# Splitting the last tile of the last product of a two-layer decoder step into two halves of the tokens

## The chip, the cores and the metric

One core of one Trainium2 chip. The metric is the device time of one execution of the program in microseconds; of several runs the median is given.

## The reference

One inference step of two decoder layers, for a prompt of 256 tokens and 8 single-token samples that share all weights: 264 tokens of 1,024 features. Each layer has a normed input projection, a mixer (attention beside a gating or pooling part), an output projection, and then a convolutional feed-forward with 2,816 inner features. A final norm follows. What matters here is the end of it:

```python
def rmsnorm(x, g):
    xf = x.astype(jnp.float32)
    y = xf * lax.rsqrt(jnp.mean(xf * xf, axis=-1, keepdims=True) + EPS)
    return (y * g).astype(x.dtype)

def conv_ffn(x, prev, norm_g, w_gate, w_up, conv_w, conv_b, w_down):
    ...
    a = jax.nn.gelu(gc) * (h @ w_up)
    return x + a @ w_down, g_all[:, -(CONV_W - 1):]
...
    y_prompt = rmsnorm(xp, final_norm)
    y_sample = rmsnorm(xs, final_norm)
```

The norm is over a token's 1,024 features, so no token needs another one's sum.

## The kernel before, in words

Features lie on the 128 partitions and tokens along the free axis. `X` holds the residual stream as 8 tiles (`KD`) of 128 features by 264 tokens (`T`). Every weight product runs through `run` (L310): the weights are 128x128 blocks, in the order of use that `_phases` writes down, and `run` walks this order. A block is loaded as part of a chunk of 16 (`raw`, L275, three chunks in the air on SP's queue), and 8 blocks at a time are split by `split` (L290) into a high and a low part of type fp32r: ScalarE copies `wh` (L306), VectorE subtracts to get `wl` (L307), three groups of 8 ahead of their use. Activations are split the same way. Each pair of output tile `m` and inner block `k` costs three matmuls of 264 columns, high by high, high by low and low by high (L329 to L331), which add up in one PSUM tile; when a tile's last block is done, `evac` is called.

The last product is `dn1`, the feed-forward's second product of layer 1: 8 output tiles of 128 features, each with 22 inner blocks (`NF`), one tile after the other. Its right-hand side is `act`, which is complete when `dn1` starts. Its `evac` is the one of `residual(..., operand=False)` (L566): VectorE adds the tile to `X` (L572), ScalarE squares it (`sq`, L386), GpSimd adds the squares up in `acc_fin` (L398), and ScalarE multiplies the tile by the final gain (L577). The last tile's square isn't added to `acc_fin`; `Norm.finish` hands both to `rstd_of` (L403), where two matmuls with a matrix of ones sum over the partitions (L406, in plain fp32, which the trace shows as two passes each) and ScalarE takes Ln and Exp (L408, L409) to get `R`, the reciprocal root for each token. Then five multiplications by `R` on VectorE (L1022), of 1, 2, 2, 2 and 1 tiles (`YD`), each with a store of its tiles behind it (L1023), in turn from SP's and ScalarE's queue.

Tiles come from pools that turn over (`sm`, `up`, and `psm` with four PSUM tiles for products). A scheduler orders each engine's instructions by its own estimate of times; so an engine's order isn't simply that of the text, but within an engine the queue is then fixed.

Of the kernel before, what the change touches and what calls it, by code (L numbers as in the profile page):

```python
# [9 lines left out]
F32 = mybir.dt.float32  # L10
# [3 lines left out]
AF = mybir.ActivationFunctionType  # L14
ALU = mybir.AluOpType
# [3 lines left out]
P = 128  # L19
D = 1024  # L20
KD = D // P
SEQ = 256
NS = 8
T = SEQ + NS
HD = 64
NH = 8
PAST = 256
# [4 lines left out]
NF = DFF // P  # L32
# [7 lines left out]
SQL = 2  # L40
XD = (1, 2, 4, 8)
WARM = 8
YD = ((0, 1), (1, 3), (3, 5), (5, 7), (7, 8))

SC0 = 9
SGL = 6
# [30 lines left out]
NEG = -1e30  # L77
SCALE = HD ** -0.5
POOLW = (2, 4, 8, 16)
# [91 lines left out]
def _consts():  # L171
# [13 lines left out]
    c, s = np.cos(ang.astype(np.float64)).astype(f), np.sin(ang.astype(np.float64)).astype(f)  # L185
    C, S = np.ones((P, T), f), np.zeros((P, T), f)
    for b in (0, 64):
# [20 lines left out]
_INS = [  # L208
    ("w", (_NB * P * P,)), ("x", (P, KD + KD * T)), ("vec", (P, _NVEC)), ("cst", _CST_ARR.shape), ("rope", (P, 2 * T)),
    ("kt0", (NPHYS, P, 512)), ("vp0", (NPHYS, P, 512)), ("kt1", (NPHYS, P, 512)), ("vp1", (NPHYS, P, 512)),  # L210
# [1 line left out]
    ("sguw", (P, 512)), ("sgub", (P, 512)), ("poolw", (P, 512)),  # L212
]
_OUTS = [
    ("y", (KD, P, T)), ("k0", (P, 4, T)), ("v0", (P, 4, T)), ("bvn", (P, 4, NS)),
    ("k1", (P, 4, T)), ("v1", (P, 4, T)), ("poolp", (P, 4, NST)), ("pools", (P, 4, NS, NST)),
    ("cv0", (P, NF, 10)), ("cv1", (P, NF, 10)), ("cs0", (P, NF, NS)), ("cs1", (P, NF, NS)),
]
# [3 lines left out]
def tile_decoder_step(ctx: ExitStack, tc: tile.TileContext, a):  # L222
    nc = tc.nc
    v, s, g, pe = nc.vector, nc.scalar, nc.gpsimd, nc.tensor
# [6 lines left out]
    sm = ctx.enter_context(tc.tile_pool(name="sm", bufs=3))  # L231
    psm = ctx.enter_context(tc.tile_pool(name="psm", bufs=MMB, space=PSUM))
    psa = ctx.enter_context(tc.tile_pool(name="psa", bufs=8 - MMB, space=PSUM))

    def f4(name, shape=(P, 4, T), dt=F32):
        return up.tile(list(shape), dt, tag="u", name=name)
# [4 lines left out]
    def hl(tiles, k):  # L241
        return tiles[k // 4][0][:, k % 4, :], tiles[k // 4][1][:, k % 4, :]

    def at(name):
        return psa.tile([P, 512], F32, tag="at", name=name)

    XG = con.tile([P, KD + KD * T], F32, name="XG")
    GAIN = XG[:, :KD]
    X = XG[:, KD:].rearrange("p (m t) -> p m t", t=T)
# [7 lines left out]
    def vec(n):  # L257
        o, w = _VEC[n]
        return VEC[:, o:o + w]
# [28 lines left out]
    pos = [0]  # L288

    def split(t):  # L290
        for tt in range(len(splits), min(t + (LOOK if pos[0] else 0), NT - 1) + 1):
            ci = chunk_of[tt]
            for c in range(ci, min(ci + 3, len(_CHUNKS))):
                raw(c)
            o = (tt * 8 - coff[ci]) * P
            src = raws[ci][:, o:o + 8 * P]
            h = wsp.tile([P, 8 * P], F32R, tag="wh", name=f"wh{tt}")
            l = wsp.tile([P, 8 * P], F32R, tag="wl", name=f"wl{tt}")
            splits[tt] = (h, l)
            if tt == 0:  # L300
                def piece(c, e, h=h, l=l, src=src):
                    c, e = c * P, e * P
                    tc.keep_in_program_order(v.tensor_copy(h[:, c:e], src[:, c:e]))
                    tc.keep_in_program_order(v.tensor_tensor(l[:, c:e], src[:, c:e], h[:, c:e].bitcast(F32), ALU.subtract))
                return piece
            s.activation(h, src, AF.Copy)  # L306
            v.tensor_tensor(l, src, h.bitcast(F32), ALU.subtract)  # L307
        return splits[t]

    def run(order, rhs, evac, hooks=None):  # L310
        hooks = sorted((hooks or {}).items())
        n = 0
        seen, left, ps = {}, {}, {}
        for m, k in order:
            left[m] = left.get(m, 0) + 1
        for m, k in order:
            i = pos[0]
            pos[0] += 1
            h, l = split(i // 8)
            c = (i % 8) * P  # L320
            if m not in ps:
                ps[m] = psm.tile([P, 512], F32, tag="mm", name=f"mm{i}")
                first = True
            else:
                first = False
            left[m] -= 1
            o = ps[m][:, :T]
            xh, xl = rhs(m, k)
            pe.matmul(o, h[:, c:c + P], xh, start=first, stop=False)  # L329
            pe.matmul(o, h[:, c:c + P], xl, start=False, stop=False)  # L330
            pe.matmul(o, l[:, c:c + P], xh, start=False, stop=left[m] == 0)  # L331
            if left[m] == 0:
                evac(m, o)
            n += 1
            while hooks and n >= 8 * (hooks[0][0] + 1):
                for f in hooks.pop(0)[1]:
                    f()

    orders = dict(_PHASES)


# [21 lines left out]
    ones = con.tile([P, P], F32, name="ones")  # L363
# [3 lines left out]
    epst = con.tile([P, 1], F32, name="epst")  # L367
# [32 lines left out]
        def finish(self):  # L400
            return rstd_of([self.acc] + self.last, 1.0 / D, self.name)

    def rstd_of(parts, scale, name):  # L403
        p = at(f"ns_{name}")
        for i, x in enumerate(parts):
            pe.matmul(p[:, :T], ones, x, start=i == 0, stop=i == len(parts) - 1)  # L406
        R = sm.tile([P, T], F32, tag="R", name=f"R_{name}", bufs=2)
        s.activation(R, p[:, :T], AF.Ln, bias=epst, scale=scale)  # L408
        s.activation(R, R, AF.Exp, scale=-0.5)  # L409
        return R  # L410

# [102 lines left out]
        g.tensor_tensor(C0[:, l], C0[:, l], t, ALU.add)  # L514
        nc.sync.dma_start(a[f"cs{l}"], CSTATE[:, l, :, 1, :])

    def ffn(l, xg, R, down_evac, hooks=None):
        cw, cb = vec("cw"), vec("cb")
        wc = lambda i, j: cw[:, (l * 3 + i) * NF + j:(l * 3 + i) * NF + j + 1]
        cvo = sm.tile([P, NF, 10], F32, tag="cvo", name=f"cvo{l}", bufs=1)  # L520
        act = [mv(f"a{l}_{i}") for i in range((NF + 3) // 4)]
        xn = [mv(f"xn{l}{i}") for i in range(2)]
        gain = vec(f"f{l}")
        half = {}

        def normalise(m):
            z = sm.tile([P, T], F32, tag="rz", name=f"xr{l}{m}", bufs=2)
            g.tensor_tensor(z, X[:, m, :], R, ALU.mult)
            operand_tile(xn[m // 4], m, z, gain[:, m:m + 1])

        def evac(m, o):
            n, j = m
            if n == "g":
                wk = f4(f"wk{l}_{j}", (P, 2, T))
                C = wk[:, 0, :]
                if j < JN:
                    G = wk[:, 1, :]
                    v.tensor_tensor(G, o, R, ALU.mult)
                else:
                    G = o  # L540
                s.activation(C, G, AF.Identity, scale=wc(2, j), bias=cb[:, l * NF + j:l * NF + j + 1])
                v.scalar_tensor_tensor(C[:, 1:SEQ], G[:, 0:SEQ - 1], wc(1, j), C[:, 1:SEQ], ALU.mult, ALU.add)  # L542
                v.scalar_tensor_tensor(C[:, 2:SEQ], G[:, 0:SEQ - 2], wc(0, j), C[:, 2:SEQ], ALU.mult, ALU.add)
                v.tensor_tensor(C[:, SEQ:T], C[:, SEQ:T], C0[:, l, j, :], ALU.add)
                s.activation(cvo[:, j, :], G[:, SEQ - 2:T], AF.Copy)
                s.activation(C, C, AF.Gelu_apprx_tanh)
                half[j] = wk
            else:
                wk = half.pop(j)
                C, A = wk[:, 0, :], wk[:, 1, :]  # L550
                if j < JN:
                    v.tensor_tensor(A, o, R, ALU.mult)
                    g.tensor_tensor(A, A, C, ALU.mult)  # L553
                else:
                    v.tensor_tensor(A, o, C, ALU.mult)
                halves(*hl(act, j), A)

        hk = Hooks()
        for m in range(KD):
            hk.at(NA + NB_ * m, normalise, m)  # L560
        run(orders[f"ff{l}"], lambda m, k: hl(xg if m[1] < JN else xn, k), evac, hk)
        nc.sync.dma_start(a[f"cv{l}"], cvo)
        lnexp()
        run(orders[f"dn{l}"], lambda m, k: hl(act, k), down_evac, hooks)

    def residual(gain, name, operand=True):  # L566
        xg = [mv(f"xg_{name}{i}") for i in range(2)] if operand else None
# [19 lines left out]
    xg = [mv(f"xg_0{i}") for i in range(2)]  # L587
    nrm = Norm("n0", True)
# [17 lines left out]
    R = nrm.finish()  # L606
# [236 lines left out]
    xg, nrm, evac = residual(vec("f0"), "f0")  # L843
    run(orders["out0"], pick([catA, catB]), evac, hk)
    R = nrm.finish()
    gelu_set()
    xg1, nrm1, evac = residual(vec("n1"), "n1")
# [9 lines left out]
    xg, R = xg1, nrm1.finish()  # L857
# [155 lines left out]
    xg, nrm, evac = residual(vec("f1"), "f1")  # L1013
    run(orders["out1"], pick([catA, catB]), evac, hk)
    R = nrm.finish()
    gelu_set()
    _, nrm, evac = residual(vec("fin"), "fin", operand=False)
    ffn(1, xg, R, evac)
    R = nrm.finish()
    for i, (m, e) in enumerate(YD):  # L1020
        x = X[:, m:e, :]
        v.tensor_tensor(x, x, R.unsqueeze(1).to_broadcast([P, e - m, T]), ALU.mult)  # L1022
        (s if i % 2 else nc.sync).dma_start(a["y"][m:e].rearrange("m p t -> p m t"), x)  # L1023


def _lay(inp):
# [62 lines left out]
```

## Time and profile before

| | |
|---|---|
| three runs | 617.85, 618.89, 619.99 us |
| median | 618.89 us |
| profiled execution | 618.47 us |
| its span, from first to last instruction | 616.4 us |
| granted TensorE clock, mean of the span | 0.996 |
| moved by DMA in the span | 121.40 MB |

The profile is of one execution. A page gives the busy time of each engine (PE is TensorE's matmuls, PEld its weight loads, DVE VectorE, ACT ScalarE, POOL GpSimd, SPq and ACTq the queues of SP and ScalarE), the chain of work that ended last, followed back from the last instruction, and the costliest groups of instructions. Other views list instructions in order of time, group them by line and shape, or give each engine's busy time in a stretch. A matmul's duration in the profile includes the way through the array; matmuls overlap, so the pace is read from start to start.

### The profile page before, as it was taken

To read this page: it belongs to the slowest core of one execution; us is meant where nothing else is said; L and a number is where in the kernel's file an instruction comes from. 1 tells how busy PE (TensorE), PEld (TensorE's weight loads), DVE (VectorE), ACT (ScalarE), POOL (GpSimd) and SP (SyncE) were. 2 spreads that over 40 slices of the span, in tenths; PEclk is the share of its full clock that TensorE was granted. 3 is DMA by queue.
4 is the path that set the end of the run, shared out by engine and by line. 5 is a ranking of instruction groups with operands and counts; after the bars stand their busy time and mean duration, and the time that the engine had idled before them with its cause. 6 is when DMAs were issued, how large, how long until landed. Compare 5 with 4: busy or idle time off the path is not lost.

```text
span 616.4 us, 12351 instructions
## 1 busy us (share of the span) xinstructions
PE 599.4 (97%) x4924; PEld 575.3 (93%) x4924; DVE 413.1 (67%) x704; ACT 350.4 (57%) x621; POOL 84.9 (14%) x111
## 2 busy tenths in 40 slices
PE   7899999999999999999999999999999999999994
PEld 5788987999999999999999997899999999999994
DVE  6986663969976676655555686396996766764441
ACT  5459763767756555644442757376765555554441
POOL 3330132324200000001110000042420000001020
PEclk9999999999999999999999999999999999999998
DMA  7995873543655445695477559944364555554502
GB/s 259 325 403 220 328 258 54 206 153 133 216 184 205 158 184 205 228 392 200 155 229 262 219 184 141 134 175 172 136 215 170 200 182 167 199 189 166 200 1 70
DMA packets 41354, 121.40 MB, mean 197 GB/s; under 512 B 17490, under 2 KB 19410, under 8 KB 29906
## 3 DMA queue, kind: packets, MB, share of 16 engines
q1 hardware_dynamic: 40178, 119.00, 59.3%
q10 hardware_dynamic: 1120, 1.63, 0.9%
q8 instruction: 38, 0.62, 0.4%
q14 instruction: 18, 0.15, 0.1%
HBM read 116.67 MB, written 3.94 MB: 196 GB/s over the span
## 4 chain that ended last, share of the span: by engine, by line
PE 84%; DVE 7%; issue 3%; DMA 2%; ACT 2%; POOL 1%; SPq 0%; DVEq 0%; ACTq 0%
PE mm L330 26%; PE mm L329 25%; PE mm L331 25%; DMA raw<-in_w 2%; DVE wl L307 2%; DVE xn_l L374 1%; PE pv_l L465 1%; PE sc L451 1%; PE pav L494 1%; PE Z L900 1%; DVE wk L542 1%; ACT wh L306 1%; PE Z L884 1%; POOL wk L553 0%; PE pt L684 0%
## 5 line engine op out<-in xcount | busy, mean ns | idle before, releaser
L307 DVE TENSOR_TENSOR wl<-raw,wh 128x1024 fp32r<-128x1024 f32 x183 | 229.4, 1255 | 129.1 <-ACT wh L306 129.0
L306 ACT ACTIVATE wh<-raw 128x1024 fp32r<-128x1024 f32 x183 | 193.7, 1059 | 182.5 <-PE mm L330 169.3
L330 PE MATMUL mm<-xn_l,wh 128*128 128x264 f32 x544 | 154.7, 284 | 1.7 <-DVE xn_l L374 1.5
L329 PE MATMUL mm<-xn_h,wh 128*128 128x264 f32 x544 | 153.8, 283 | 0.0
L331 PE MATMUL mm<-xn_h,wl 128*128 128x264 f32 x544 | 153.4, 283 | 0.0
L330 PEld LDWEIGHTS mm<-xn_l,wh 128*128 128x128 f32 x544 | 102.3, 188 | 2.5 <-DVE xn_l L374 2.5
L329 PEld LDWEIGHTS mm<-xn_h,wh 128*128 128x128 f32 x544 | 102.1, 188 | 0.0
L331 PEld LDWEIGHTS mm<-xn_h,wl 128*128 128x128 f32 x544 | 102.1, 188 | 0.0
L330 PE MATMUL mm<-a_l,wh 128*128 128x264 f32 x352 | 99.8, 284 | 0.0
L329 PE MATMUL mm<-a_h,wh 128*128 128x264 f32 x352 | 99.5, 284 | 0.0
L331 PE MATMUL mm<-a_h,wl 128*128 128x264 f32 x352 | 99.4, 283 | 0.0
L331 PEld LDWEIGHTS mm<-a_h,wl 128*128 128x128 f32 x352 | 66.2, 188 | 0.0
L330 PEld LDWEIGHTS mm<-a_l,wh 128*128 128x128 f32 x352 | 66.2, 188 | 0.0
L329 PEld LDWEIGHTS mm<-a_h,wh 128*128 128x128 f32 x352 | 66.0, 188 | 0.0
L329 PE MATMUL mm<-xg_h,wh 128*128 128x264 f32 x160 | 46.6, 298 | 3.6 <-DVE q L637 1.6
L330 PE MATMUL mm<-xg_l,wh 128*128 128x264 f32 x160 | 46.1, 293 | 0.0
L331 PE MATMUL mm<-xg_h,wl 128*128 128x264 f32 x160 | 44.7, 291 | 1.3 <-DVE wl L307 1.3
L329 PE MATMUL mm<-xg_f_h,wh 128*128 128x264 f32 x160 | 45.8, 286 | 0.0
L330 PE MATMUL mm<-xg_f_l,wh 128*128 128x264 f32 x160 | 45.4, 284 | 0.0
L331 PE MATMUL mm<-xg_f_h,wl 128*128 128x264 f32 x160 | 45.3, 283 | 0.0
L329 PE MATMUL mm<-xg_n_h,wh 128*128 128x264 f32 x128 | 37.4, 292 | 0.0
L331 PE MATMUL mm<-xg_n_h,wl 128*128 128x264 f32 x128 | 36.8, 288 | 0.0
(266 smaller groups left out, 1074.5 us busy)
## 6 DMA issues: line engine op xcount, KB each, us to landing
raw<-in_w SPq DMA_DIRECT2D x89, 1024.0 KB, 4.8
K<-in_kt SPq DMA_DIRECT2D x32, 256.0 KB, 6.0
V<-in_vp SPq DMA_DIRECT2D x32, 256.0 KB, 5.6
raw<-in_w SPq DMA_DIRECT2D x5, 512.0 KB, 5.3
CST<-in_cst SPq DMA_DIRECT2D x1, 548.0 KB, 5.5
XG<-in_x ACTq DMA_DIRECT2D x1, 528.0 KB, 7.8
out_k<-k SPq DMA_DIRECT2D x1, 528.0 KB, 9.4
out_v<-v SPq DMA_DIRECT2D x1, 528.0 KB, 3.0
```

Of the source, the lines that this page charges most:

```text
L306: s.activation(h, src, AF.Copy)
L307: v.tensor_tensor(l, src, h.bitcast(F32), ALU.subtract)
L329: pe.matmul(o, h[:, c:c + P], xh, start=first, stop=False)
L330: pe.matmul(o, h[:, c:c + P], xl, start=False, stop=False)
L331: pe.matmul(o, l[:, c:c + P], xh, start=False, stop=left[m] == 0)
L374: j = v.scalar_tensor_tensor(l, src, gain, h.bitcast(F32), ALU.mult, ALU.subtract)
L451: pe.matmul(ps[32 * t:32 * t + 32, :PAST].rearrange("p (g k) -> p g k", g=NPG), qz[:, t, sq, :], kt[sq][:, :, t * P:(t + 1) * P], start=sq ...
L465: pe.matmul(pv[32 * j:32 * j + 32, :], pz[:, pg, sq, :], vtiles[sq][:, pg, :], start=pg == 0, stop=pg == NPG - 1)
L494: pe.matmul(o, vt[:, 0, h * HD:(h + 1) * HD], w[:, :SEQ], start=True, stop=False)
L542: v.scalar_tensor_tensor(C[:, 1:SEQ], G[:, 0:SEQ - 1], wc(1, j), C[:, 1:SEQ], ALU.mult, ALU.add)
L884: tc.keep_in_program_order(pe.matmul(ps[:, 0:SEQ], kh[:, 0:P], qh[:, 0:SEQ], start=False, stop=False, skip_group_check=True))
L900: pe.matmul(ps[:, 0:384], negU, x, start=False, stop=False, skip_group_check=True)
```

## The change

The last tile of `dn1` (its 22 blocks) leaves `run` and goes through a new function, twice: once for tokens 0 to 131 and once for tokens 132 to 263 (`HT` = 132). Each half has a PSUM tile of its own, its own add, square and gain, its own sum over partitions and `R`, and its own four multiplications and stores. In the first half the square and `acc` are added on VectorE before one sum; in the second the sum takes both, as before. The multiplications write to a new tile `Y` instead of in place, two feature tiles of 132 tokens at a time (264 elements for a partition), and the output `y` is laid out so that a store's piece for one partition, two tiles by 132 tokens, is contiguous.

```diff
+HT = T // 2
-YD = ((0, 1), (1, 3), (3, 5), (5, 7), (7, 8))
+YD = ((0, 2), (2, 4), (4, 6), (6, 8))
-    ("y", (KD, P, T)), ("k0", (P, 4, T)), ("v0", (P, 4, T)), ("bvn", (P, 4, NS)),
+    ("y", (2, P, KD, HT)), ("k0", (P, 4, T)), ("v0", (P, 4, T)), ("bvn", (P, 4, NS)),
+    def run_last(order, rhs, evac):
+        base = pos[0]
+        pos[0] += len(order)
+        for hf in range(2):
+            a_, b_ = hf * HT, (hf + 1) * HT
+            ps = psm.tile([P, 512], F32, tag="mm", name=f"last{hf}")
+            o = ps[:, :HT]
+            for n, (m, k) in enumerate(order):
+                h, l = split((base + n) // 8)
+                c = ((base + n) % 8) * P
+                xh, xl = [x[:, a_:b_] for x in rhs(m, k)]
+                pe.matmul(o, h[:, c:c + P], xh, start=n == 0, stop=False)
+                pe.matmul(o, h[:, c:c + P], xl, start=False, stop=False)
+                pe.matmul(o, l[:, c:c + P], xh, start=False, stop=n == len(order) - 1)
+            evac(hf, o)
...
-    def rstd_of(parts, scale, name):
+    def rstd_of(parts, scale, name, n=T):
...
-            pe.matmul(p[:, :T], ones, x, start=i == 0, stop=i == len(parts) - 1)
+            pe.matmul(p[:, :n], ones, x, start=i == 0, stop=i == len(parts) - 1)
...
-        s.activation(R, p[:, :T], AF.Ln, bias=epst, scale=scale)
+        s.activation(R, p[:, :n], AF.Ln, bias=epst, scale=scale)
...
-        run(orders[f"dn{l}"], lambda m, k: hl(act, k), down_evac, hooks)
+        rhs = lambda m, k: hl(act, k)
+        if last is None:
+            run(orders[f"dn{l}"], rhs, down_evac, hooks)
+        else:
+            run(orders[f"dn{l}"][:-NF], rhs, down_evac, hooks)
+            run_last(orders[f"dn{l}"][-NF:], rhs, last)
...
-    ffn(1, xg, R, evac)
-    R = nrm.finish()
-    for i, (m, e) in enumerate(YD):
-        x = X[:, m:e, :]
-        v.tensor_tensor(x, x, R.unsqueeze(1).to_broadcast([P, e - m, T]), ALU.mult)
-        (s if i % 2 else nc.sync).dma_start(a["y"][m:e].rearrange("m p t -> p m t"), x)
+    def last(hf, o):
+        tok = slice(hf * HT, (hf + 1) * HT)
+        m = KD - 1
+        x = X[:, m, tok]
+        v.tensor_tensor(x, x, o, ALU.add)
+        q = sm.tile([P, HT], F32, tag="sq", name=f"sq_last{hf}")
+        s.activation(q, x, AF.Square)
+        s.activation(x, x, AF.Copy, scale=vec("fin")[:, m:m + 1])
+        acc = nrm.acc[:, tok]
+        if hf == 0:
+            v.tensor_tensor(q, q, acc, ALU.add)
+        R = rstd_of([q] if hf == 0 else [acc, q], 1.0 / D, f"fin{hf}", HT)
+        Y = f4(f"y{hf}", (P, KD, HT))
+        for i, (m, e) in enumerate(YD):
+            v.tensor_tensor(Y[:, m:e], X[:, m:e, tok], R.unsqueeze(1).to_broadcast([P, e - m, HT]), ALU.mult)
+            (s if i % 2 else nc.sync).dma_start(a["y"][hf, :, m:e, :], Y[:, m:e])
+    ffn(1, xg, R, evac, last=last)
```

More of the change, by code (lines that the diff above doesn't have):

```diff
@@ L401, in finish @@
             return rstd_of([self.acc] + self.last, 1.0 / D, self.name)
-    def rstd_of(parts, scale, name):
+    def rstd_of(parts, scale, name, n=T):
         p = at(f"ns_{name}")
         for i, x in enumerate(parts):
-            pe.matmul(p[:, :T], ones, x, start=i == 0, stop=i == len(parts) - 1)
-        R = sm.tile([P, T], F32, tag="R", name=f"R_{name}", bufs=2)
-        s.activation(R, p[:, :T], AF.Ln, bias=epst, scale=scale)
+            pe.matmul(p[:, :n], ones, x, start=i == 0, stop=i == len(parts) - 1)
+        R = sm.tile([P, n], F32, tag="R", name=f"R_{name}", bufs=2)
+        s.activation(R, p[:, :n], AF.Ln, bias=epst, scale=scale)
         s.activation(R, R, AF.Exp, scale=-0.5)
@@ L515, in conv_prep, with ffn @@
         nc.sync.dma_start(a[f"cs{l}"], CSTATE[:, l, :, 1, :])
-    def ffn(l, xg, R, down_evac, hooks=None):
+    def ffn(l, xg, R, down_evac, hooks=None, last=None):
         cw, cb = vec("cw"), vec("cb")
@@ L1068 @@
     o = {n: np.asarray(r.results[0]["out_" + n]) for n, _ in _OUTS}
-    y = o["y"].transpose(2, 0, 1).reshape(T, D)
+    y = o["y"].transpose(0, 3, 2, 1).reshape(T, D)
     def kv(k, w):
```

## The prediction

> **What bounds the kernel now.** I read the page first (busy shares, then the chain that ended last), then stretches of the last 17 us, then that stretch in order of time.
>
> ```profile
> span 616.4 us, 12351 instructions
> ...
> PE 599.4 (97%) x4924; PEld 575.3 (93%) x4924; DVE 413.1 (67%) x704; ACT 350.4 (57%) x621; POOL 84.9 (14%) x111
> ...
> PE 84%; DVE 7%; issue 3%; DMA 2%; ACT 2%; POOL 1%; SPq 0%; DVEq 0%; ACTq 0%
> ```
>
> TensorE is busy 97% of the span and holds 84% of the chain that ended last. So a microsecond more on TensorE is a microsecond more of time, unless something behind TensorE shrinks. Only the end of the program lies behind it.
>
> ```profile
> core 0: us, PE busy (x) PEld busy (x) DVE busy (x) ACT busy (x) POOL busy (x), PEclk, DMA share, GB/s
> 599.20:607.10 7.90, 7.90 (x68) 7.90 (x67) 0.43 (x1) 0.94 (x2) 0.75 (x1) 1.00 0.00 0
> ...
> 610.10:612.80 2.70, 0.00 (x0) 0.00 (x0) 2.63 (x5) 0.00 (x0) 0.00 (x0) 0.72 0.40 135
> 612.80:616.40 3.60, 0.00 (x0) 0.00 (x0) 0.00 (x0) 0.00 (x0) 0.00 (x0) 0.50 0.57 200
> ```
>
> The first stretch is the last tile of the last product: TensorE never stops, at granted clock 1.00, and the weights are long there (DMA share 0). The other two are the multiplications by R and the stores. Their DMA shares give 0.40 x 2.70 + 0.57 x 3.60 = 3.13 us in which all 16 engines are full, for the 1,056 KB of y. The stages in order of time (start, duration, engine):
>
> ```profile
> 599.21 0.28 PE L329 MATMUL mm<-a_h,wh 128*128 128x264 f32 x1
> ...
> 607.07 0.28 PE L331 MATMUL mm<-a_h,wl 128*128 128x264 f32 x1
> ...
> 607.39 0.43 DVE L572 TENSOR_TENSOR XG<-XG,mm 128x264 f32<-128x264 f32 x1 [7.55 <-PE mm L331]
> 607.92 0.42 ACT L386 ACTIVATE sq_fin<-XG 128x264 f32<-128x264 f32 x1 [7.01 <-DVE XG L572]
> ...
> 608.39 0.71 PE L406 MATMUL ns_fin<-sq_fin,ones 128*128 128x264 f32 x2 [0.59 <-ACT sq_fin L386]
> 609.14 0.48 ACT L408 ACTIVATE R_fin<-ns_fin,epst 128x264 f32<-128x264 f32 x1 [0.26 <-PE ns_fin L406]
> 609.65 0.42 ACT L409 ACTIVATE R_fin<-R_fin 128x264 f32<-128x264 f32 x1
> 610.11 2.63 DVE L1022 TENSOR_TENSOR XG<-XG,R_fin 128x264 f32<-128x264 f32 x5 [2.29 <-ACT R_fin L409]
> ...
> 612.81 0.34 SPq L1023 DMA_DIRECT2D out_y<-XG  x1
> ```
>
> The last tile has 22 blocks x 3 products = 66 matmuls; the first starts at 599.21, the last at 607.07, so 65 steps take 7.86 us and one takes 0.121 us. From the start of the last matmul to the first multiplication are 610.11 - 607.07 = 3.04 us, from there to the end of the span 616.4 - 610.11 = 6.29. This tail of 9.33 us is a strict chain, and it is what the change can shorten.
>
> **The change part by part.** Engine by engine the changed program's order equals the old one, apart from buffer and line numbers, until the last tile; nothing earlier moves, on SP's and POOL's queues either.
>
> (1) *TensorE.* 66 matmuls of 264 columns become 132 of 132 columns. The columns are the same in all, but each matmul brings its own weight load (the page counts 4,924 of both), so the loads double. Does a 132-column matmul take half of 0.121, or is the load the floor? No 132-column one is in the trace; the nearest rows are two.
>
> ```profile
> 66.23 0.98 PEld L724 LDWEIGHTS pO<-ow,CST 128*128 128x128 f32 x8
> 67.13 0.19 PEld L329 LDWEIGHTS mm<-xg_h,wh 128*128 128x128 f32 x1
> ```
>
> At L724 eight matmuls of only 8 columns follow one another, each with a full 128x128 load. The load behind them starts at 67.13: (67.13 - 66.23)/8 = 0.1125 us each. With almost nothing to stream, that is the pace of loads.
>
> ```profile
> 351.54 0.22 PE L901 MATMUL Z<-Lh,nonesr 128*128 128x128 f32 x1
> ...
> 352.07 0.22 PE L901 MATMUL Z<-Ll,nonesr 128*128 128x128 f32 x1
> ...
> 351.54 0.19 PEld L330 LDWEIGHTS mm<-xg_n_l,wh 128*128 128x128 f32 x1
> 351.65 0.19 PEld L331 LDWEIGHTS mm<-xg_n_h,wl 128*128 128x128 f32 x1
> ...
> 352.07 0.19 PEld L329 LDWEIGHTS mm<-xg_n_h,wh 128*128 128x128 f32 x1
> 352.18 0.19 PEld L330 LDWEIGHTS mm<-xg_n_l,wh 128*128 128x128 f32 x1
> ```
>
> L901 is a 128-column matmul in the same type (fp32r) as the last product. The next load starts with it, at 351.54 and 352.07; the load after that, which can begin once its predecessor is in and in use, starts 0.11 us later both times. So a matmul of about half the columns gives way to the next after 0.11 us, not 0.06. I take **0.111 us**, between the two rows. The ends are 0.0605 (half of 0.121, loads free) and 0.121 (a half as dear as a whole).
>
> The Trainium skill bears on this twice, on its page "TensorE: Matmul & The Clock Gate". Its section "LDWEIGHTS (loading the stationary operand)" gives columns / 1.2 ns, 107 ns for 128, whatever is streamed; by that the change costs TensorE 131 x 0.107 + 0.22 - 7.86 = 6.4 us. Its section "Back-to-back issue gap" gives about 81 ns per matmul for a sustained stream at 128 columns; by that it costs 131 x 0.081 + 0.22 - 7.86 = 3.0 us. The rows at L724 and L901 side with the first.
>
> From the first half's first matmul to the second half's last are 131 steps: 131 x 0.111 = 14.54 us. Into the second half's stream falls the first half's sum over partitions, two fp32 passes of 132 columns, at a load each 0.22. Together 14.76, against 7.86: **+6.90 us**.
>
> (2) *Hidden part.* Half 0's chain (add, square, add of acc, sum, R, four multiplications, four stores) runs beside half 1's matmuls. Its sum stands behind 30 of them in TensorE's order, 30 x 0.111 = 3.3 us after the first half's end; the chain up to it is by the rows above about 0.3 (to the add) + 0.5 + 0.5 + 0.4 = 1.7 us, so TensorE doesn't wait there. R is ready some 1.3 us after that (0.5 + 0.4 + 0.4), the four multiplications end about 6.1 us after the half's last matmul, and half 1 takes 66 x 0.111 + 0.22 = 7.5. Behind ScalarE's two store issues stands half 1's square, behind VectorE's multiplications half 1's add: both free about a microsecond early. Cost nothing; without that margin, its overrun would be added.
>
> (3) *Half 1's chain up to R.* Each step handles 132 columns. What half the columns save:
>
> ```profile
> L414 DVE TENSOR_TENSOR catA_l<-pav,catA_h 128x256 fp32r<-128x256 f32 x8 | 3.4, 421 | 10.9 <-ACT catA_h L413 10.4 <-issue 0.5
> ...
> L746 DVE TENSOR_TENSOR tril<-tril,CST 128x128 f32<-128x128 f32 x1 | 0.3, 270 | 0.0
> ...
> L675 ACT ACTIVATE p<-p,st 128x256 f32<-128x256 f32 x8 | 4.0, 505 | 0.0
> ...
> L674 ACT ACTIVATE p<-p,st 128x128 f32<-128x128 f32 x8 | 3.2, 399 | 0.0
> ```
>
> 128 columns fewer save 0.421 - 0.270 = 0.15 us on VectorE (one add) and 0.505 - 0.399 = 0.11 on ScalarE (square, Ln, Exp: 0.33). The sum's two passes over the square save 0.11 each (0.22; 264 columns in two fp32 passes are 0.22 of the 0.71), the last matmul's own streaming 0.05. The pass over acc runs under the add and the square, as now. Saved: 0.05 + 0.15 + 0.33 + 0.22 = **0.75 us**.
>
> (4) *Multiplications and stores of half 1.*
>
> ```profile
> L1022 DVE TENSOR_TENSOR XG<-XG,R_fin 128x528 f32<-128x528 f32 x3 | 1.9, 700 | 0.0
> L1022 DVE TENSOR_TENSOR XG<-XG,R_fin 128x264 f32<-128x264 f32 x2 | 0.9, 429 | 2.3 <-ACT R_fin L409 2.3
> ...
> out_y<-XG ACTq DMA_DIRECT2D x2, 264.0 KB, 2.2
> ...
> out_y<-XG SPq DMA_DIRECT2D x2, 132.0 KB, 1.7
> ```
>
> Alone the five sum to 3 x 0.70 + 2 x 0.43 = 2.96, in the chain they take 2.63: 0.08 overlaps at each joint. Four of 264 elements (two rows of 132) thus take 3 x 0.35 + 0.43 = 1.48 instead of 2.63. The last store now goes out at 612.81, 0.07 after the last multiplication, and the span ends 3.59 later. Its engines are full then: loaded stores land in 2.2, the median of the two 132 KB ones is 1.7, so 0.5 us of the 3.59 is queueing (bounds 0 and 0.7). In half 1 only 528 KB remain, 3.13/2 = 1.57 us of data, that start after the first of four multiplications; the queue drains as fast as they come. I take the 0.5 as gone. New: 1.48 + 0.07 + 3.59 - 0.5 = 4.64, against 6.29: **1.65 us** saved (1.15 to 1.85). A store's pieces stay 1,056 bytes (264 x 4 before, 2 x 132 x 4 after).
>
> Sum: +6.90 - 0.75 - 1.65 = **+4.5 us**. The profiled execution took 618.47 us (its span of 616.4 and 2.07 around it) and would take 622.97; the median of the three runs shown is 618.89, 0.42 above, and by it I forecast **623.4 us**, 0.7% slower. The whole yield of the split is 2.4 us, and TensorE pays 6.9 for it.
>
> **The rivals.**
>
> A. *A half costs as much as a whole* (the step stays 0.121, since load and swap set it already). For: it is only 0.01 above the load's pace. Against: both rows above are below it. 131 x 0.121 + 0.22 - 7.86 = 8.21, less 2.40: +5.8, **624.7**.
>
> B. *The loads hide* and the halves stream at 0.0605. TensorE then pays 131 x 0.0605 + 0.22 - 7.86 = 0.29, less 2.40, and about 0.2 comes back, since half 0's multiplications would end 1.8 (30 steps) + 1.3 (sum to R) + 1.5 = 4.6 us after that half, with half 1's add due behind them at 66 x 0.0605 + 0.22 + 0.2 = 4.4: -1.9, **617.0**, at the 0.3% bound on the faster side. It decides from a step of (7.86 + 2.40 - 0.22)/131 = 0.077 us downwards, since there the two prices are equal. For: steady matmuls run as fast as their columns would. Against: L901 at 0.11.
>
> C. *Loads are quicker in a long stream.* Loads are not all equal:
>
> ```profile
> L331 PEld LDWEIGHTS mm<-a_h,wl 128*128 128x128 f32 x352 | 66.2, 188 | 0.0
> ...
> L684 PEld LDWEIGHTS pt<-CST,p 128*128 128x128 f32 x24 | 2.7, 140 | 0.4 <-issue 0.4
> ```
>
> Were these paced like the 140 ns ones, 0.111 x 140/188 = 0.083: 131 x 0.083 + 0.22 - 7.86 = 3.23, less 2.40, +0.8, **619.7**. The Trainium skill's 81 ns, from the section named above, would come out here as well. Against: the last product's loads are the 188 ones.
>
> D. *The tail gives nothing back*: half 0's chain overruns, or the last store takes its 3.59 as before and the engines' fixed parts eat the rest. +6.9, **625.8**. Against: margins of about a microsecond in (2).
>
> **How the numbers follow.** Forecast 0.80, A 0.08, B 0.04, C 0.04, D 0.04. The load's two rows (0.109 to 0.1125) move the sum by 0.2 to 0.3 us, the queueing by 0.2 to 0.5, and the three runs of before lie within 1.1 us of their median; with A inside, the range is 621.8 to 625.1. About 0.3% (1.9 us) is what a measurement of this kernel can tell from no change. Slower by more: the forecast, A, D: 0.91 (a little of the forecast's lower edge is lost). Within: C and half of B: 0.06. Faster: half of B: 0.03.
>
> **What would show it.** In the changed profile the last tile's matmuls should start every 0.11 us, from 599.2 to about 613.9; half 0's sum should stand among half 1's matmuls with no idle time before it, and half 0's stores should be done before the last matmul or soon after. From the last matmul to the first multiplication 2.3 us, from there to the end 4.6. A step near 0.06 would make the forecast wrong on the faster side, a step of 0.12 or more, or a drop of the granted clock below 1.00 while the loads keep the array half idle, on the slower one.

## The result, and the profile after

| | before | after |
|---|---|---|
| runs | 5 | 5 |
| median | 618.89 us | 623.49 us |
| lowest, highest | 617.85, 620.50 | 622.41, 624.85 |
| profiled execution | 618.47 us | 622.66 us |
| its span | 616.4 us | 620.5 us |

The change makes the kernel slower by 0.7%: the ratio is 1.0071, with a 95% interval of 1.0054 to 1.0088. The medians are 4.60 us apart; forecast were 4.5.

From the page of the changed kernel, the busy shares and the chain that ended last. The products' lines L329 to L331 are L330 to L332 here, and the last tile's matmuls stand at L352 to L354. (Matmuls and loads in fp32r are printed as f32.)

```profile
span 620.5 us, 12500 instructions
...
PE 606.3 (98%) x4992; PEld 582.9 (94%) x4992; DVE 413.8 (67%) x709; ACT 351.4 (57%) x625; POOL 84.7 (14%) x111
...
PE 84%; DVE 7%; issue 3%; ACT 2%; DMA 2%; POOL 1%; SPq 0%; ACTq 0%; DVEq 0%
```

TensorE has 6.9 us more of busy time, 68 more matmuls and as many more loads (66 for the tile, 2 for the extra sum). The other engines have hardly changed.

The same kernel in order of time: the ends of the split tile, the first half's sum among the second half's matmuls, and the tail.

```profile
598.91 0.23 PE L352 MATMUL last<-a_h,wh 128*128 128x132 f32 x1
...
609.36 0.28 PE L353 MATMUL last<-a_l,wh 128*128 128x132 f32 x1
609.47 0.27 PE L354 MATMUL last<-a_h,wl 128*128 128x132 f32 x1
609.58 0.44 PE L424 MATMUL ns_fin<-sq_last,ones 128*128 128x132 f32 x2
609.77 0.31 PE L352 MATMUL last<-a_h,wh 128*128 128x132 f32 x1
...
613.72 0.27 PE L354 MATMUL last<-a_h,wl 128*128 128x132 f32 x1
...
614.03 0.29 DVE L1045 TENSOR_TENSOR XG<-XG,last 128x132 f32<-128x132 f32 x1 [1.75 <-PE last L354]
614.41 0.31 ACT L1047 ACTIVATE sq_last<-XG 128x132 f32<-128x132 f32 x1 [3.64 <-DVE XG L1045]
...
614.78 0.49 PE L424 MATMUL ns_fin<-sq_last,ones 128*128 128x132 f32 x2 [0.51 <-ACT sq_last L1047]
615.31 0.37 ACT L426 ACTIVATE R_fin<-ns_fin,epst 128x132 f32<-128x132 f32 x1
615.71 0.31 ACT L427 ACTIVATE R_fin<-R_fin 128x132 f32<-128x132 f32 x1
616.06 1.46 DVE L1055 TENSOR_TENSOR y<-XG,R_fin 128x264 f32<-128x264 f32 x4 [1.74 <-ACT R_fin L427]
```

Read three distances. From the tile's first matmul to its last are 613.72 - 598.91 = 14.81 us (7.86 before). From there to the first multiplication of half 1 are 2.34 us (3.04 before), and from that to the end of the span 620.5 - 616.06 = 4.4 to 4.5 us (6.29 before). The matmuls start 0.11 us apart, and the sum of half 0 stands between two of them at that pace: nothing waits for it.

One distance carries the comparisons below: from the last tile's first matmul to the end of the span. What lies ahead of it is the same program text in all these kernels, yet the tile's first matmul started anywhere between 598.5 and 600.0 us in their profiles. So the times scatter by a microsecond where this distance does not: 17.2 us before, 21.6 after, and 21.7 when the change was profiled a second time.

| kernel | distance, us | median of its runs, us | before beside it, us | ratio, 95% interval |
|---|---|---|---|---|
| before | 17.2 | | | |
| the change | 21.6 | 623.49 | 618.89 | 1.0071 (1.0054 to 1.0088) |
| e1 products in halves | 23.8 | 624.45 | 619.24 | 1.0087 (1.0069 to 1.0105) |
| e2 200 and 64 tokens | 25.3 | 626.9 | 619.24 | 1.0106 (1.0072 to 1.0140) |
| e3 64-column loads | 15.8 | 617.82 (one run) | 619.24 | |
| e4 bf16 | 15.7 | 617.76 (one run) | 619.24 | |
| e5 tail in halves | 17.6 | 618.1 | 618.61 | 0.9993 (0.9984 to 1.0001) |
| e6 the change again | 21.7 | 622.65 | 618.61 | 1.0069 (1.0055 to 1.0083) |
| e7 as e1 | 23.7 | 624.96 | 618.61 | 1.0104 (1.0089 to 1.0119) |
| e8 164 and 100 tokens | 21.2 | 622.55 (one run) | 618.61 | |
| e9 as e5, SP's queue | 18.0 | 619.36 | 618.63 | 1.0007 (0.9994 to 1.0021) |
| e10 as e5, six stores | 16.4 | 618.45 | 618.63 | 0.9988 (0.9974 to 1.0002) |

### The profile page after: what moved, and what is told of

The parts are those of the page before. It is cut to its first block, busy times and chain, and to the rows that moved or that the text cites. A ratio compares the mean times of both kernels' runs of the same rounds, so it can differ in the third digit from the quotient of the medians.

```text
span 620.5 us, 12500 instructions
## 1 busy us (share of the span) xinstructions
PE 606.3 (98%) x4992; PEld 582.9 (94%) x4992; DVE 413.8 (67%) x709; ACT 351.4 (57%) x625; POOL 84.7 (14%) x111
## 4 chain that ended last, share of the span: by engine, by line
PE 84%; DVE 7%; issue 3%; ACT 2%; DMA 2%; POOL 1%; SPq 0%; ACTq 0%; DVEq 0%
PE mm L331 25%; PE mm L330 25%; PE mm L332 25%; DVE wl L308 2%; DVE xn_l L392 1%; PE pv_l L483 1%; PE sc L469 1%; DMA XG<-in_x 1%; DMA raw<-in_w 1%; PE last L354 1%; PE last L353 1%; PE last L352 1%; PE pav L512 1%; PE Z L923 1%; DVE wk L560 1%
## 5 line engine op out<-in xcount | busy, mean ns | idle before, releaser
L331 PE MATMUL mm<-xn_l,wh 128*128 128x264 f32 x544 | 154.8, 284 | 1.7 <-DVE xn_l L392 1.5
L330 PE MATMUL mm<-xn_h,wh 128*128 128x264 f32 x544 | 153.8, 283 | 0.0
L332 PE MATMUL mm<-xn_h,wl 128*128 128x264 f32 x544 | 153.4, 283 | 0.0
L331 PEld LDWEIGHTS mm<-xn_l,wh 128*128 128x128 f32 x544 | 102.3, 188 | 2.5 <-DVE xn_l L392 2.5
L330 PEld LDWEIGHTS mm<-xn_h,wh 128*128 128x128 f32 x544 | 102.1, 188 | 0.0
L332 PEld LDWEIGHTS mm<-xn_h,wl 128*128 128x128 f32 x544 | 102.1, 188 | 0.0
L331 PE MATMUL mm<-a_l,wh 128*128 128x264 f32 x330 | 93.5, 284 | 0.0
L330 PE MATMUL mm<-a_h,wh 128*128 128x264 f32 x330 | 93.3, 284 | 0.0
L332 PE MATMUL mm<-a_h,wl 128*128 128x264 f32 x330 | 93.2, 283 | 0.0
L332 PEld LDWEIGHTS mm<-a_h,wl 128*128 128x128 f32 x330 | 62.1, 188 | 0.0
L331 PEld LDWEIGHTS mm<-a_l,wh 128*128 128x128 f32 x330 | 62.0, 188 | 0.0
L330 PEld LDWEIGHTS mm<-a_h,wh 128*128 128x128 f32 x330 | 61.9, 188 | 0.0
L330 PE MATMUL mm<-xg_h,wh 128*128 128x264 f32 x160 | 46.8, 299 | 3.7 <-ACT wh L307 2.2
L331 PE MATMUL mm<-xg_l,wh 128*128 128x264 f32 x160 | 45.9, 293 | 0.0
L330 PE MATMUL mm<-xg_f_h,wh 128*128 128x264 f32 x160 | 45.8, 286 | 0.0
L331 PE MATMUL mm<-xg_f_l,wh 128*128 128x264 f32 x160 | 45.4, 284 | 0.0
L332 PE MATMUL mm<-xg_h,wl 128*128 128x264 f32 x160 | 45.2, 295 | 0.1
L332 PE MATMUL mm<-xg_f_h,wl 128*128 128x264 f32 x160 | 45.3, 283 | 0.0
L330 PE MATMUL mm<-xg_n_h,wh 128*128 128x264 f32 x128 | 37.4, 292 | 0.0
L332 PE MATMUL mm<-xg_n_h,wl 128*128 128x264 f32 x128 | 36.8, 288 | 0.0
```

## The experiments

A matmul here has weight columns (the block that is loaded, 128 columns) and moving columns (the tokens that are streamed against it, 264 or 132); its step is the time from its start to the next one's. The theory: the step of the split matmuls is set by the load of their 128 fp32r weight columns, so the split costs TensorE 6.9 us, and the split tail gives 2.4 back. The rivals: a matmul has a price of its own, whatever it loads; the columns set the step; the split tail gives nothing.

### e3 and e4: what sets the step

In e3 64 weight columns, so that half of the tile's features are left out of the result (this edit and the next are against the change):

```diff
-            o = ps[:, :HT]
+            o = ps[:64, :HT]
-                pe.matmul(o, h[:, c:c + P], xh, start=n == 0, stop=False)
+                pe.matmul(o, h[:, c:c + 64], xh, start=n == 0, stop=False)
...
-        v.tensor_tensor(x, x, o, ALU.add)
+        v.tensor_tensor(x[:64], x[:64], o, ALU.add)
```

In e4 the upper 16 bits of both operands, read as bf16:

```diff
+                w_, v_ = [z[:, c:c + P].bitcast(BF16)[:, 1::2] for z in (h, l)]
+                xh, xl = [z.bitcast(BF16)[:, 1::2] for z in (xh, xl)]
+                pe.matmul(o, w_, xh, start=n == 0, stop=False)
...
```

> The change with 64 weight columns for each matmul of the last tile instead of 128 (the tile's other 64 features are left out of the product). Theory (the load's 128 columns set the step): the load takes half as long, 0.056, and the step becomes that of the stream of 132 columns, 0.06 to 0.07 us; the tile takes 8 to 9.5 us, the span is 5 to 6.5 us shorter than the change's. Rival (a fixed price of a matmul with a load): step 0.112, span as the change's.

> The change with the last tile's matmuls reading the upper 16 bits of weights and activations as bf16 (every second element; the lower bits are left out). Theory (the load of a 32-bit weight column sets the step): a 16-bit load is quicker, the step falls to between 0.06 and 0.085 us and the tile to 8 to 11.4 us. Rival (a fixed price of a matmul with a load, or of its 128 columns in any type): step 0.112, tile 14.8 us.

Stretches of the last tile's instructions alone, first of the change (the columns are the stretch, its length, busy time and count of PE, PEld and DVE, granted clock, DMA share and GB/s), then of e3.

```profile
599.00:606.20 7.20, 7.20 (x66) 7.20 (x66) 0.00 (x0) 1.00 0.01 2
```

```profile
600.00:604.00 4.00, 4.00 (x67) 4.00 (x67) 0.00 (x0) 1.00 0.02 4
```

Three starts of e4 one after the other:

```profile
602.00 0.22 PE L354 MATMUL last<-a_h,wh 128*128 128x132 bf16 x1
602.06 0.22 PE L355 MATMUL last<-a_l,wh 128*128 128x132 bf16 x1
602.12 0.22 PE L356 MATMUL last<-a_h,wl 128*128 128x132 bf16 x1
```

About 66 matmuls of 132 columns take 7.2 us with the full load and 4.0 us with half of it: 0.062 us from start to start with 64 columns of weights, at the same count of matmuls and the same moving columns. With 16-bit weights and all 128 columns the step is 0.06 as well. The loads of the two kernels say why:

```profile
L353 PEld LDWEIGHTS last<-a_l,wh 128*64 128x64 f32 x43 | 5.8, 136 | 0.0
```

```profile
L355 PEld LDWEIGHTS <-wh 128*128 128x128 bf16 x43 | 4.2, 97 | 0.0
```

In the change the same load is this:

```profile
L353 PEld LDWEIGHTS last<-a_l,wh 128*128 128x128 f32 x44 | 8.4, 192 | 0.0
```

A load of 192 ns takes 136 ns with half the columns and 97 ns in bf16. These durations are longer than the steps, so loads overlap, and only their order is compared here. So a matmul has no fixed price of 0.112, and its 128 weight columns as such have none either; it is the load of 128 columns of 32 bits. (e4 makes the moving columns 16-bit too. e2 below speaks against these setting the step: with 200 moving columns it is the same as with 132.) Once the load is out of the way, halves cost halves: the distance is 15.8 and 15.7 us, 1.4 to 1.5 less than before, each in one profiled execution. That is the world of rival B, in which the change would have paid.

### e1, e7 and e6: products and tail taken apart

e1 and e7 are the same kernel: the products in halves as in the change, then the tail of before, with one norm for all tokens and five multiplications and stores. e6 is the change once more. The edit is against the change:

```diff
     def last(hf, o):
...
+        x = X[:, KD - 1, hf * HT:(hf + 1) * HT]
         v.tensor_tensor(x, x, o, ALU.add)
...
     ffn(1, xg, R, evac, last=last)
+    nrm.add(KD - 1)
+    x = X[:, KD - 1, :]
+    s.activation(x, x, AF.Copy, scale=vec("fin")[:, KD - 1:KD])
+    R = nrm.finish()
+    for i, (m, e) in enumerate(YD):
+        x = X[:, m:e, :]
+        v.tensor_tensor(x, x, R.unsqueeze(1).to_broadcast([P, e - m, T]), ALU.mult)
...
```

> The last tile's products in two halves of 132 tokens as in the change, but one norm and the five multiplications and stores of before. Theory (weight loads set the step of the halves at 0.112 us, and the split tail gives 2.4 us back): 131 x 0.112 = 14.7 us of products instead of 7.9, so +6.8, and 0.2 less for the smaller last add and matmul; about 6.6 us slower than before, that is 625.5 us, 2 us slower than the change. Rival (the split tail gives nothing and the change lost only what its products lose): the same as the change, 623.5 us.

> The products in halves with the tail of before once more, on the same chip as the change. Theory: from the tile's first matmul to the end of the span 23.7 us, and 2.0 to 2.2 us slower than the change in the same call. Rival (the split tail gives nothing back): level with the change.

> The changed kernel once more, to stand beside the other runs of this call: 4.4 us more than before; from the tile's first matmul to the end of the span 21.6 us.

From the profile of e7, in order of time, the first and the last matmul of the tile and the multiplications:

```profile
598.47 0.23 PE L352 MATMUL last<-a_h,wh 128*128 128x132 f32 x1
```

```profile
613.05 0.27 PE L354 MATMUL last<-a_h,wl 128*128 128x132 f32 x1
```

```profile
615.94 1.67 DVE L1052 TENSOR_TENSOR XG<-XG,R_fin 128x264 f32<-128x264 f32 x3 [2.29 <-ACT R_fin L427]
```

The products take 613.05 - 598.47 = 14.58 us without the sum among them (the change has 14.81 with it: the sum costs 0.23). The tail then is the old one: 615.94 - 613.05 = 2.89 us to the first multiplication, and 622.2 - 615.94 = 6.3 to the end. The distance is 23.8 us in e1 and 23.7 in e7, as expected. In times, e1 lay 5.2 us above its kernel before, 1.4 less than the 6.6 expected, and the change was not measured beside it. Measured side by side the three stand in order: 618.61, 622.65 (the change) and 624.96 (e7). The split tail is worth 2.3 us in time and 2.1 in distance. The rival that it gives nothing is out; e1's time by itself, without the change beside it, had left room for it.

### e2 and e8: other cuts

```diff
-HT = T // 2
+CUT = (0, 200, T)
...
-            a_, b_ = hf * HT, (hf + 1) * HT
+            a_, b_ = CUT[hf], CUT[hf + 1]
```

In e8 `CUT` is `(0, 164, T)`.

> The change with 200 and 64 tokens instead of 132 and 132. Theory (the step is the weight load's): 0.112 us for matmuls of 200 columns and for those of 64, 14.8 us for the tile as in the change; the tail behind it is shorter by about 1 us (64 columns a step, a quarter of the stores), 622.5 us. Rival (columns set the step): about 0.170 for 200 columns and 0.054 for 64 if the 0.112 of 132 columns were theirs, the products still 14.8 in sum but in unequal parts.

> The change with 164 and 100 tokens. In the run with 64 tokens the array streamed for 27 of 112 ns a step and the granted clock fell to a half; with 132 it streams for 55 and the clock stayed. Here it streams for 42 of 112. If what counts is the share of time in which columns stream, with the limit near a quarter, the clock stays at 1.00 and the steps at 0.112, the tile at 14.8 us; if the limit is near a half, the second part's steps go to 0.21 us after about 3 us of it.

Stretches of the last tile's instructions in e2: the 200-column part, then two of the 64-column part (the same columns as above).

```profile
599.70:606.90 7.20, 7.20 (x66) 7.20 (x66) 0.00 (x0) 1.00 0.01 2
```

```profile
607.20:609.60 2.40, 2.40 (x24) 2.40 (x23) 0.31 (x1) 1.00 0.01 3
610.00:618.70 8.70, 8.34 (x39) 8.28 (x39) 0.00 (x0) 0.50 0.27 94
```

The 200-column matmuls take the same 7.2 us for 66 as the 132-column ones, and the first 64-column ones the same again: about 0.11 each (24 begun or ended in 2.40 us). Three widths, one step; the columns do not set it. Then, at 609.8 us, the granted clock falls to 0.50, and the steps double to 0.213. The second part takes 11.8 us, and the kernel comes out 4.4 us later than expected, though the tail behind it is shorter (3.7 us from the first multiplication to the end, 4.4 in the change; about 1 us less was expected). Not every execution lost as much: of the four, three took 626.8 to 627.0 us at a mean granted clock of 0.985, and one 623.36 us at 0.991. In e8 nothing of the kind happened in the products:

```profile
606.80:614.10 7.30, 7.23 (x66) 7.13 (x65) 0.33 (x1) 1.00 0.18 65
```

100 columns a step kept the clock at 1.00 and the tile at 14.8 us, in the one execution of e8. So at a step of 0.112 us, the clock fell with 64 columns and held with 100. That it is the small share of streaming which lets it fall is argued from these two and the change, not shown by itself; where between them the limit lies, and how it is counted, these runs don't tell. The Trainium skill, on its page "TensorE: Matmul & The Clock Gate" in Part 1, describes a gate that sets the clock by how busy TensorE has been and halves it after an idle window. The trace agrees in the size of the step (1.00 to 0.50), and adds that a TensorE which never waits (busy 2.40 of 2.40 us just before) can fall under it.

### e5, e9 and e10: the tail alone

In e5 the products are whole again, two adds, squares, sums and R follow, and GpSimd multiplies the last tile by the gain (against the change):

```diff
+        for hf, tok in enumerate(toks):
+            x = X[:, m, tok]
+            v.tensor_tensor(x, x, o[:, tok], ALU.add)
+            q = sm.tile([P, HT], F32, tag="sq", name=f"sq_last{hf}")
+            tc.keep_in_program_order(s.activation(q, x, AF.Square))
+            g.tensor_tensor(x, x, vec("fin")[:, m:m + 1].to_broadcast([P, HT]), ALU.mult)
...
+        tc.keep_in_program_order(s.activation(R, p, AF.Ln, bias=epst, scale=1.0 / D))
+        tc.keep_in_program_order(s.activation(R, R, AF.Exp, scale=-0.5))
...
```

On top of it, in e9 all eight stores go out on SP's queue:

```diff
-            (s if i % 2 else nc.sync).dma_start(a["y"][hf, :, m:e, :], Y[:, m:e])
+            nc.sync.dma_start(a["y"][hf, :, m:e, :], Y[:, m:e])
```

And in e10 instead six stores, three for each half:

```diff
-YD = ((0, 2), (2, 4), (4, 6), (6, 8))
+YD = ((0, 2), (2, 5), (5, 8))
```

> The last tile's products as before (66 matmuls of 264 columns), but the tail behind them in two halves of the tokens: two adds, two squares, two sums and two R (the first half's Exp ahead of the second's Ln), eight multiplications of 264 elements and eight stores; the gain of the last tile is multiplied in by GpSimd beside them. Theory (the split of the tail is worth something by itself, the products' split is pure loss): the first multiplication comes 2.3 us after the last matmul instead of 3.04, the stores start 0.7 us earlier and then keep the DMA engines busy without a gap; 1.0 us less than before from the last matmul on, 618.2 us for 619.2. Rival (only the overlap with matmuls made the tail shorter): nothing gained, 9.3 us from the last matmul as before.

> The tail alone in halves, with all eight stores on SP's queue. In the profile of the run before with a tail in halves, the data of y was out 1.0 us earlier than in the kernel before, but the last store's completion came 1.0 us after its last packet; an 8 KB instruction fetch stood between that store's last data packet and its 4-byte completion packet on one DMA engine. Theory (the fetch held the completion up, and it is ScalarE's, drawn by the instructions of its stores): no fetch inside the tail, completion about 0.15 us after the last packet, 8.4 us from the last matmul to the end of the span instead of 9.3, 0.9 us less than before. Rival (it is another engine's fetch, or the completion of the last store is late for another reason): 9.3 to 9.7 us again, level with before.

> The tail alone in halves, with six stores (2, 3 and 3 tiles for each half) in turn on SP's and ScalarE's queues instead of eight. Theory: fewer instructions on both queues and on VectorE, no fetch inside the tail or an earlier one; the engines are full from the first store on, so the data is out as early; 8.4 to 8.6 us from the last matmul to the end, 0.8 us less than before. Rival: 9.3 us, level with before.

In e5 the last matmul of 264 columns starts at 606.88 us. In order of time, the multiplications; then stretches (busy time of PE, PEld, DVE, ACT and POOL, granted clock, DMA share, GB/s):

```profile
609.23 2.84 DVE L1068 TENSOR_TENSOR y<-XG,R_fin 128x264 f32<-128x264 f32 x8 [1.54 <-ACT R_fin L1063]
```

```profile
613.60:614.00 0.40, 0.00 (x0) 0.00 (x0) 0.00 (x0) 0.00 (x0) 0.00 (x0) 0.50 0.21 71
614.00:616.60 2.60, 0.00 (x0) 0.00 (x0) 0.00 (x0) 0.00 (x0) 0.00 (x0) 0.50 0.00 0
```

R comes earlier as expected (2.35 us after the last matmul instead of 3.04), and the data of y is out by 614.0, against 615.0 in the kernel before. But the span goes on for 2.6 us, where the kernel before has 1.4. So from the last matmul to the end are 9.7 us: not the 8.3 that the theory gave, and longer even than the rival's 9.3. What the DMA engines did in the half microsecond around 614:

```profile
q14 instruction: 1, 0.01, 3.9%
q10 hardware_dynamic: 3, 0.00, 1.3%
```

One instruction fetch ran there, beside the last three packets of ScalarE's stores. My theory for e9 was that this fetch is ScalarE's and goes away with its stores. It did not: e9 has as many fetches of that queue as e5 (19, one more than before), one of them at 614.0 us in its tail, and its distance is 18.0 us. So that theory fell. One queue was also slower at moving the data: 275 to 282 GB/s where two queues moved 352. The eight stores went out from 610.19 to 613.57, one in 0.48 us, and 132 KB in 0.48 us are 280 GB/s, so the pace of issue accounts for this rate. In e10 no fetch fell into the tail:

```profile
613.60:614.00 0.40, 0.00 (x0) 0.00 (x0) 0.00 (x0) 0.00 (x0) 0.00 (x0) 0.50 0.48 178
614.00:615.50 1.50, 0.00 (x0) 0.00 (x0) 0.00 (x0) 0.00 (x0) 0.00 (x0) 0.50 0.00 0
```

The data is out at the same time, the span ends 1.5 us later, and the distance is 16.4 us, 0.75 less than before: what the theory said for e10. In times it is 0.9988 of before (0.9974 to 1.0002), and e5 0.9993 (0.9984 to 1.0001): both intervals include no change. The tail in halves with the products left whole is the only kind of version in full precision that isn't slower than before; that one of its kind is faster is seen in the profile of one execution, not in the times. A fetch in the tail goes with a late store: from issue to landing, the slowest store of y took 3.2 us in e5 and 3.0 in e9, the two profiles with such a fetch, and at most 2.6 in the ten others. Why it does stays open, as does whose fetch it is.

## Why the prediction was right, point by point

**TensorE.** The step was put at 0.111 us, between the loads at L724 (0.1125) and the 128-column matmul at L901 (0.11). It is 0.112 in both halves (0.111 on the average of all steps, since the first took 0.06), and the tile takes 14.81 us for 14.76 forecast. e3, e4, e2 and e8 show the reason to be the one given: the step follows the load's columns and type, and not the moving columns from 64 to 200.

**The hidden part.** Half 0's sum stood behind 30 matmuls of half 1 and added 0.23 us (0.22 forecast). Its multiplications began at 610.81 and took 1.46, so they ended 1.8 us ahead of half 1's add at 614.03: the margin was larger than the microsecond given.

**The chain up to R** gave 3.04 - 2.34 = 0.70 us for 0.75. VectorE, ScalarE and the sum gave what was worked out (0.15, 0.33 and 0.22). For the sum the working is not clean: it puts the two passes over 264 columns at 0.22 us together, half of which would be 0.11. Each of the two passes became 0.11 us shorter (386 to 276 and 490 to 379 ns), as its other words say. The 0.05 of the last matmul's own streaming did not come: from its start to the add are 0.31 us, 0.32 before.

**Multiplications and stores** gave 6.29 - 4.44 = 1.85 us for 1.65, the upper bound of what was given. The four multiplications took 1.46 for 1.48. The rest is what the prediction called queueing, taken as 0.5 and found about 0.7, its upper bound: from the last store's issue to the end are 2.9 us (617.6 to 620.5) for 3.59. The stores were all in within 1.9 us, and none took 2.2 any more:

```profile
DMA to landing us min/median/max: 1.8/1.9/1.9
```

**Sum.** 14.81 - 7.86 = 6.95, less 0.70 and 1.85: 4.4 us by the profiles, 4.5 forecast, 4.6 between the medians. The cost came 0.05 higher than forecast, the first saving 0.05 lower and the second 0.20 higher; that they partly cancel is luck, but each is small beside the 6.9.

**Rivals.** A (a half costs a whole) and B (the loads hide) fall with the step of 0.112. C needed quicker loads: in the change they took 192 ns, no less than the 188 of before; only e4's bf16 ones, of 97 ns, were quicker. D (the tail gives nothing) falls with e6 and e7 side by side. The last sentence of the prediction named a drop of the granted clock; at 132 columns it did not come (1.00 through the tile), at 64 it did.

## What to carry to other kernels

Splitting a product by its moving columns doubles its weight loads, and here a load of 128 columns in fp32r set a step of 0.112 us, nearly as long as that of a matmul of 264 columns (0.121), so the split nearly doubled the tile (7.86 to 14.81 us); look for two loads in a row behind a narrow matmul in the trace before pricing a split by its columns. Price the overlap that it buys from the tail's own rows: here 2.55 us against 6.95. And when only the tail is to be shorter, leave the product whole: splitting the tail alone was level with before here, and no gain in time was shown.

## What the runs showed of the hardware that was not expected

A TensorE that had work without a gap lost its clock: with 64 moving columns in a step of 0.112 us the granted clock fell from 1.00 to 0.50 about 2.9 us into the stretch (606.95 to 609.8), and both loads and matmuls went to steps of 0.213 us. With 100 columns it held, in one execution.

The tile's last store can end the span late though its data is out early: in e5 2.6 us passed from there to the end, against 1.4 in the kernel before, and in its profile an instruction fetch ran at that moment. What links the two is not shown.
